# Turning a residual to tokens on partitions: tensor-engine transposes, or VectorE 32x32 transposes with DMAs through DRAM

## The chip, the core and the metric

The kernel runs on one core of a Trainium2 chip. The metric is the device time of one execution in microseconds; the runs shown before the change have a median of 2171.61 us (three runs, 2171.5 to 2172.09).

Engine names are those of the profile: PE is the tensor engine's matmul and PEld its weight load, DVE is VectorE, ACT is ScalarE, POOL is GpSimd, SP is the engine that issues most DMAs. Each engine works through its own instructions in a fixed order. Where an instruction waits, everything behind it on that engine waits too.

## What is computed

A decoder trunk of two residual layers on 256 tokens of width 2048, in float32. The second layer is what matters here:

```python
h = h + odd_mixer(rms_norm(h, mix_norm_w[1]), ...)
f = conv_ffn(rms_norm(h, ffn_norm_w[1]), ...)      # silu(conv(hn @ w_gate)) * (hn @ w_up) @ w_down
h = h + f
return rms_norm(h, final_norm_w)
```

`w_gate` and `w_up` are 2048 x 5632, `w_down` is 5632 x 2048. The output has tokens on the rows.

## The kernel before, in words

**The residual.** `h` stays in SBUF in four tiles `h0` to `h3` (`self.hq`), each of 128 partitions by 4 x 256 floats. Through most of the program a partition is a channel and the 256 columns of a block are tokens. The last down-projection (`finish`) produces tokens on partitions, so before it `h` has to be turned. That is the work of `turn` (L416), a generator that is started with the second layer's FFN (L856) and is not needed until `finish` adds into `h`.

**The products.** Gate and up (`products`, L263) are made of 44 jobs of 256 output channels, each of four weight panels of 512 KB; this text numbers the panels of the second layer from 0. Panels 0 to 7 are the first gate job and the first up job, alternating; from then on a job is four panels in a row: 8 to 11 gate, 12 to 15 up, 16 to 19 gate, 20 to 23 up, 24 to 27 gate, 28 to 31 up, and so on. For a panel, SP loads `raw` (L165, four buffers), ACT rounds it to its high part in `hl` (L167, three buffers), DVE computes the low part as the difference (L168), and PE runs sixteen matmuls (L243): for each of two accumulators and four slices of the panel, one with the high part over 512 columns and one with the low part over 256.

**Behind a job.** Each accumulator is emptied by `total`: ACT copies its upper half (`ev`, L302), DVE adds the lower half (L303). A gate job goes on with a DVE multiplication into a padded tile `pad` (L869), ACT's scaling `cv` (L872), two DVE steps of the convolution (L873, L874), ACT's SiLU (L875) and POOL's multiplication (L876). An up job goes on with DVE's product with that `cv` (L886) and with the split into `act` (ACT L388, DVE L389).

**What sets the order.** `tick` (L292) advances every waiting generator by one step after each panel. The order in which instructions then stand on each engine is not that of the source alone: a scheduler of the framework places them when the program is built, by the order of the source and its own costs. A changed step can so move its neighbours.

**The norm.** `token_scale` runs behind panel 2 (statistics, L335) and panel 4 (broadcast on PE, L343); between them DVE has a chain of ten small steps (L319 to L325).

**The turn before.** From the thirteenth tick on, every fourth tick turns one 128-token half of one tile:

```python
for i in range(4):
    self.nc.tensor.transpose(ps[:, i * P : (i + 1) * P], block[:, i], self.ident)
self.nc.scalar.copy(block, ps.rearrange("p (i c) -> p i c", c=P))
```

That is four 128x128 transposes on PE (L425) into one PSUM bank and one ACT copy back over the block (L426), eight times.

Of the kernel before, what the change touches and what calls it, by code (L numbers as in the profile page):

```python
# [9 lines left out]
F32 = mybir.dt.float32  # L10
# [5 lines left out]
P = 128  # L16
T = 256
NT = T // P
# [54 lines left out]
class Trunk:  # L73
# [341 lines left out]

    def turn(self):  # L416

        for _ in range(12):
            yield
        for g in range(WG):  # L420
            for tt in range(NT):
                ps = self.psum()
                block = self.hq[g][:, :, tt * P : (tt + 1) * P]
                for i in range(4):
                    self.nc.tensor.transpose(ps[:, i * P : (i + 1) * P], block[:, i], self.ident)  # L425
                self.nc.scalar.copy(block, ps.rearrange("p (i c) -> p i c", c=P))  # L426
                yield
                yield
                yield
                yield  # L430

    def pair_sums(self, a0, a1, lent=None, lend=False, homes=None):

# [1067 lines left out]
```

## Time and profile before

| | |
|---|---|
| Median of the runs shown | 2171.61 us |
| Time of the profiled execution | 2171.28 us |
| Its span in the profile | 2169.5 us |
| PE busy, share of the span | 100% |
| DVE, ACT busy, share of the span | 77%, 57% |
| Mean granted TensorE clock | 0.999 |

The span is what the profile records of the program's instructions; the 1.8 us between the profiled execution's span and its time lie before and after. In the profile a busy share says how full an engine is. A group's row has the line, the engine, the operation, what it writes and reads, the count, the busy time, the mean duration in ns, and the idle time ahead of it with what ended it. In a timeline the first two numbers are the start and the length of a piece, and a bracket tells how long the engine had been idle and for whom.

### The profile page before, as it was taken

To read this page: it belongs to the slowest core of one execution; us is meant where nothing else is said; L and a number is where in the kernel's file an instruction comes from. 1 tells how busy PE (TensorE), PEld (TensorE's weight loads), DVE (VectorE), ACT (ScalarE), POOL (GpSimd) and SP (SyncE) were. 2 spreads that over 40 slices of the span, in tenths; PEclk is the share of its full clock that TensorE was granted. 3 is DMA by queue.
4 is the path that set the end of the run, shared out by engine and by line. 5 is a ranking of instruction groups with operands and counts; after the bars stand their busy time and mean duration, and the time that the engine had idled before them with its cause. 6 is when DMAs were issued, how large, how long until landed. Compare 5 with 4: busy or idle time off the path is not lost.

```text
span 2169.5 us, 35606 instructions
## 1 busy us (share of the span) xinstructions
PE 2160.1 (100%) x13723; PEld 1948.6 (90%) x13723; DVE 1679.1 (77%) x2712; ACT 1226.6 (57%) x1855; POOL 96.8 (4%) x107
## 2 busy tenths in 40 slices
PE   9999999999999999999999999999999999999998
PEld 8888888888888888899989999888888888888998
DVE  8788776766676668789889998767666666688997
ACT  7556554655555555555556665546555555555554
POOL 0000000101010100000000000000010101000000
PEclk9999999999999999999999999999999999999999
DMA  7754556556655565566555555555555655666665
GB/s 263 235 175 146 175 183 189 191 194 194 195 194 194 194 194 191 191 200 207 186 193 186 185 174 195 166 194 185 186 193 194 194 194 195 194 203 199 210 200 169
DMA packets 117722, 417.65 MB, mean 193 GB/s; under 512 B 13072, under 2 KB 15408, under 8 KB 117552
## 3 DMA queue, kind: packets, MB, share of 16 engines
q1 hardware_dynamic: 116352, 412.48, 58.3%
q8 instruction: 107, 1.75, 0.3%
q0 software_dynamic: 576, 2.10, 0.3%
q10 hardware_dynamic: 624, 0.81, 0.1%
q14 instruction: 63, 0.52, 0.1%
HBM read 413.22 MB, written 2.11 MB: 191 GB/s over the span
## 4 chain that ended last, share of the span: by engine, by line
PE 99%; DVE 0%; DMA 0%; ACT 0%; SPq 0%; issue 0%; DVEq 0%
PE acc L243 68%; PE acc L578 10%; PE acc L527 6%; PE aux L542 4%; PE acc L542 4%; PE acc L253 1%; PE aux L527 1%; PE acc L260 1%; PE acc L204 0%; PE aux L978 0%; PE aux L1010 0%; PE acc L212 0%; PE aux L212 0%; PE aux L1000 0%; DMA raw<-in_wfirst 0%; PE aux L1311 0%
## 5 line engine op out<-in xcount | busy, mean ns | idle before, releaser
L243 PE MATMUL acc<-x,hl 128*128 128x512 f32 (+1 forms) x7680 | 1325.8, 334 | 0.0
L243 PEld LDWEIGHTS acc<-x,hl 128*128 128x128 f32 x7680 | 1158.5, 188 | 150.2 <-issue 0.9
L168 DVE TENSOR_TENSOR hl<-raw,hl 128x1024 fp32r<-128x1024 f32 x687 | 840.2, 1223 | 410.1 <-ACT hl L167 404.3
L167 ACT CAST hl<-raw 128x1024 fp32r<-128x1024 f32 x687 | 721.3, 1050 | 617.0 <-PE acc L243 364.7
L578 PE MATMUL acc<-hl,act 128*128 128x256 f32 x1872 | 223.7, 277 | 0.0
L578 PEld LDWEIGHTS acc<-hl,act 128*128 128x128 f32 x1872 | 218.5, 188 | 0.6
L243 PE MATMUL acc<-o,hl 128*128 128x512 f32 (+1 forms) x1024 | 176.0, 333 | 0.0
L302 ACT COPY ev<-acc 128x256 f32<-128x256 f32 x242 | 89.9, 372 | 149.3 <-PE acc L243 148.3
L243 PEld LDWEIGHTS acc<-o,hl 128*128 128x128 f32 x1024 | 154.4, 188 | 19.9
L876 POOL TENSOR_TENSOR cv<-cv,rbc 128x256 f32<-128x256 f32 x88 | 93.6, 1083 | 852.7 <-ACT cv L875 852.7
L527 PE MATMUL acc<-hl,act 128*128 128x512 f32 x528 | 120.1, 389 | 0.0
L527 PEld LDWEIGHTS acc<-hl,act 128*128 128x128 f32 x528 | 99.0, 188 | 20.5
L303 DVE TENSOR_TENSOR ev<-acc,ev 128x256 f32<-128x256 f32 x242 | 101.1, 420 | 3.5 <-ACT ev L302 1.9
L506 ACT CAST ts<-tf 128x768 fp32r<-128x768 f32 x77 | 64.3, 836 | 45.0 <-DVE tf L503 44.6
L508 DVE TENSOR_TENSOR ts<-tf,ts 128x768 fp32r<-128x768 f32 x77 | 73.3, 952 | 2.3 <-ACT ts L506 2.2
L496 ACT CAST hl<-raw 128x768 fp32r<-128x768 f32 x53 | 44.3, 836 | 29.2 <-issue 12.2
L500 DVE TENSOR_TENSOR tf<-raw 128x512 f32<-128x512 f32 x77 | 53.1, 690 | 9.7 <-DMA raw<-in_wd 7.9
L542 PE MATMUL aux<-ts,x 128*128 128x256 f32 x405 | 54.6, 276 | 0.0
L542 PE MATMUL acc<-hl,act 128*128 128x256 f32 x318 | 53.4, 276 | 0.0
L505 DVE TENSOR_TENSOR hl<-raw,hl 128x768 fp32r<-128x768 f32 x53 | 50.5, 952 | 3.1 <-ACT hl L496 2.3
L542 PEld LDWEIGHTS aux<-ts,x 128*128 128x128 f32 x405 | 49.9, 188 | 0.0
L886 DVE TENSOR_TENSOR ev<-ev,cv 128x256 f32<-128x256 f32 x88 | 38.3, 437 | 10.3 <-POOL cv L876 1.6
(278 smaller groups left out, 1687.9 us busy)
## 6 DMA issues: line engine op xcount, KB each, us to landing
raw<-in_wg SPq DMA_DIRECT2D x176, 512.0 KB, 3.5
raw<-in_wu SPq DMA_DIRECT2D x176, 512.0 KB, 3.5
raw<-in_wd SPq DMA_DIRECT2D x176, 512.0 KB, 4.1
raw<-in_wev SPq DMA_DIRECT2D x76, 512.0 KB, 4.1
raw<-in_wod SPq DMA_DIRECT2D x64, 512.0 KB, 3.9
raw<-in_wevo SPq DMA_DIRECT2D x32, 512.0 KB, 3.8
raw<-in_wodv SPq DMA_DIRECT2D x32, 512.0 KB, 3.6
raw<-in_wodo SPq DMA_DIRECT2D x32, 512.0 KB, 3.6
```

Of the source, the lines that this page charges most:

```text
L167: nc.scalar.copy(hi, raw)
L168: self.lo = nc.vector.tensor_tensor(lo, raw, hi.bitcast(F32), ALU.subtract)
L243: self.mm = self.nc.tensor.matmul(accs[nt][:, :n], hl[w][:, k, nt * P : (nt + 1) * P], xs[k0 + k][:, :n], start=start and k == w == 0, sto ...
L302: nc.scalar.copy(t, acc[:, T:])
L303: nc.vector.tensor_tensor(t, acc[:, :T], t, ALU.add)
L500: v.tensor_tensor(two(blk(f123, 0, 2)), two(blk(raw, 1, 2)), blk(raw, 3).unsqueeze(1).broadcast_to([P, 2, T]), ALU.subtract)
L506: nc.scalar.copy(t123[0], f123)
L508: v.tensor_tensor(t123[1], f123, t123[0].bitcast(F32), ALU.subtract)
L527: self.nc.tensor.matmul(row.rearrange("p (j c) -> p j c", c=T), self.part(a[k], p, tt), self.both(hl, w, k), start=start and i == k == 0, ...
L542: self.nc.tensor.matmul(to, x[p], w[b][q], start=n == 0 and i in start, stop=n == 2 and i in stop, skip_group_check=alone or i in m,)
L578: mm(row[:, j * T : (j + 1) * T] if own is None else own[:, :T], x, w[:, j], start=first, stop=stop and k == 1 and i == 2 and j == halves[-1],
L876: nc.gpsimd.tensor_tensor(c, c, self.rbc, ALU.mult)
```

## The change

`turn` no longer uses PE, PSUM or ACT's copy. For each of the four tiles:

- one DVE instruction (`nc.vector.transpose`, STREAM_TRANSPOSE in the order below) transposes every 32x32 block of the 128 x 1024 tile into a tile `tr`, of which there is one buffer;
- one DMA, issued by ACT, writes `tr` to a DRAM tile `turn` (512 KB);
- three ticks later four DMAs, issued by ACT, read it back so that each 32x32 block comes to its place; each fills 32 partitions of `h` (128 KB) in 1024 pieces of 128 bytes.

```diff
+        nc = self.nc
         for _ in range(12):
             yield
         for g in range(WG):
-            for tt in range(NT):
-                ps = self.psum()
-                block = self.hq[g][:, :, tt * P : (tt + 1) * P]
-                for i in range(4):
-                    self.nc.tensor.transpose(ps[:, i * P : (i + 1) * P], block[:, i], self.ident)
-                self.nc.scalar.copy(block, ps.rearrange("p (i c) -> p i c", c=P))
+            h = self.hq[g].rearrange("p i t -> p (i t)")
+            t = self.t256("tr", 1, 4 * T)
+            nc.vector.transpose(t, h)
+            back = self.dram.tile([P, 4 * T], F32, name=f"turn{g}")
+            nc.scalar.dma_start(back, t)
+            for _ in range(3):
                 yield
-                yield
-                yield
-                yield
+            src = back.rearrange("(p r) (i b c) -> b r i p c", r=32, b=4, c=32)
+            for b in range(4):
+                dst = h[32 * b : 32 * b + 32].rearrange("r (i p c) -> r i p c", p=4, c=32)
+                nc.scalar.dma_start(dst, src[b])
+            yield
```

The scheduler places the new instructions by its own costs, and with them their neighbours on ACT and DVE up to panel 32; from there on all engines stand as before. In the new kernel the lines of the source behind `turn` are three higher (L872 is L875, L875 is L878). The rows below are ACT's; a name's number tells the tiles of one kernel apart.

**Behind panel 19 (the end of a gate job).** Before, in ACT's order, from the cast of panel 19 (`hl_15415`) over those of panels 20, 21 and 22; the two L302 empty the accumulators of panels 16 to 19:

```order
L167 CAST hl_15415<-raw_15414 128x1024
L426 COPY h_88<-aux_15367 128x4x128
L167 CAST hl_15459<-raw_15458 128x1024
L167 CAST hl_15486<-raw_15485 128x1024
L302 COPY ev_15436<-acc_15344 128x256
L302 COPY ev_15446<-acc_15345 128x256
L167 CAST hl_15507<-raw_15506 128x1024
```

Now, again on ACT from the cast of panel 19 (`hl_15416`); panel 20 is `hl_15463`:

```order
L167 CAST hl_15416<-raw_15415 128x1024
L432 DMA h_89<-turn_15371 32x32x32 x2
L302 COPY ev_15436<-acc_15346 128x256
L302 COPY ev_15446<-acc_15347 128x256
L167 CAST hl_15463<-raw_15462 128x1024
L426 DMA turn_15485<-tr_15483 128x1024
```

The casts of panels 20 and 21 stood ahead of the two copies that empty the accumulators of panels 16 to 19; now they stand behind them.

**Behind panel 23 (the end of an up job).** Before, on ACT, from the cast of panel 24 (`hl_15563`); the L302 empty the accumulators of panels 20 to 23:

```order
L167 CAST hl_15563<-raw_15562 128x1024
L167 CAST hl_15590<-raw_15589 128x1024
L302 COPY ev_15548<-acc_15456 128x256
L302 COPY ev_15554<-acc_15457 128x256
L167 CAST hl_15611<-raw_15610 128x1024
L388 CAST act_14856<-ev_15548 128x256
L388 CAST act_14857<-ev_15554 128x256
```

Now, on ACT from the cast of panel 23 (`hl_15530`) to that of panel 24 (`hl_15569`):

```order
L167 CAST hl_15530<-raw_15529 128x1024
L432 DMA h_90<-turn_15485 32x32x32 x2
L302 COPY ev_15550<-acc_15460 128x256
L432 DMA h_90<-turn_15485 32x32x32
L388 CAST act_14856<-ev_15550 128x256
L302 COPY ev_15556<-acc_15461 128x256
L432 DMA h_90<-turn_15485 32x32x32
L388 CAST act_14857<-ev_15556 128x256
L167 CAST hl_15569<-raw_15568 128x1024
```

Here the cast of panel 24 stands behind both copies, two DMAs and both of the job's `act` casts.

**Behind panel 27 (the end of a gate job).** Before, on ACT, from the cast of panel 28 (`hl_15675`):

```order
L167 CAST hl_15675<-raw_15674 128x1024
L167 CAST hl_15702<-raw_15701 128x1024
L302 COPY ev_15652<-acc_15560 128x256
L302 COPY ev_15662<-acc_15561 128x256
L167 CAST hl_15723<-raw_15722 128x1024
L872 ACTIVATE cv_15656<-pad_14899,params 128x256
L872 ACTIVATE cv_15666<-pad_14900,params 128x256
```

Now, on ACT from the cast of panel 27 (`hl_15636`) to those of panels 28 (`hl_15683`) and 29:

```order
L167 CAST hl_15636<-raw_15635 128x1024
L432 DMA h_91<-turn_15591 32x32x32 x2
L302 COPY ev_15656<-acc_15566 128x256
L302 COPY ev_15666<-acc_15567 128x256
L432 DMA h_91<-turn_15591 32x32x32
L875 ACTIVATE cv_15660<-pad_14899,params 128x256
L875 ACTIVATE cv_15670<-pad_14900,params 128x256
L167 CAST hl_15683<-raw_15682 128x1024
L167 CAST hl_15704<-raw_15703 128x1024
```

The cast of panel 28 now follows both copies and both scalings of the job that panel 27 ends.

Three smaller moves, in words. On ACT the cast of panel 9 stood between the copies of panels 0 to 6 and those of panel 7's job; now it stands behind all four copies, and behind it come the table load, the first SiLU, a scaling and the cast of panel 10. On DVE the transposition of `h2` stands between the low part of panel 14 and that of panel 15, and waits for the write of `turn1`, which ACT issues behind the cast of panel 14. On PE each of panels 10, 20, 24 and 28 now begins with two matmuls over 512 columns, one for each accumulator, before the first that needs the low part; before, each began with one.

## Prediction

> **What bounds the kernel now.** I begin with the page: span, engines, and the chain of waits that ended last.
>
> ```profile
> span 2169.5 us, 35606 instructions
> PE 2160.1 (100%) x13723; PEld 1948.6 (90%) x13723; DVE 1679.1 (77%) x2712; ACT 1226.6 (57%) x1855; POOL 96.8 (4%) x107
> PE 99%; DVE 0%; DMA 0%; ACT 0%; SPq 0%; issue 0%; DVEq 0%
> ```
>
> PE never stops, and the chain is PE's own work. Whatever leaves PE shortens the run; whatever makes PE wait lengthens it. Next the stretch in which the transposes stand, by engine, and the transposes by their line:
>
> ```profile
> 1483.00:1563.00 80.00, 80.00 (x481) 71.08 (x481) 53.82 (x80) 45.62 (x72) 7.15 (x8) 1.00 0.57 187
> L425 PE MATMUL aux<-consts,h x32: 272/272/273, 1483.6 to 1563.3; 128*128 128x128 f32 x32
> L426 ACT COPY h<-aux x8: 577/581/582, 1484.8 to 1564.2; 128x512 f32<-128x512 f32 x8
> ```
>
> In these 80 us PE is busy throughout, at a granted clock of 1.00, while DVE works 53.82 us and ACT 45.62: a third of each is free on average. That average is not yet a reason: ACT and DVE prepare the panels, in order. What counts is how early. ACT's timeline around the first transposes:
>
> ```profile
> 1479.75 0.37 ACT L302 COPY ev<-acc 128x256 f32<-128x256 f32 x1 [0.27 <-PE acc L243]
> 1481.11 0.38 ACT L302 COPY ev<-acc 128x256 f32<-128x256 f32 x1 [0.99 <-PE acc L243]
> 1481.38 1.05 ACT L167 CAST hl<-raw 128x1024 fp32r<-128x1024 f32 x1
> 1482.33 0.91 ACT L872 ACTIVATE cv<-pad,params 128x256 f32<-128x256 f32 x2
> 1483.88 1.05 ACT L167 CAST hl<-raw 128x1024 fp32r<-128x1024 f32 x1 [0.64 <-ACT cv L872]
> ```
>
> and PE's timeline:
>
> ```profile
> 1461.77 22.03 PE L243 MATMUL acc<-x,hl 128*128 128x512 f32 x128
> 1483.63 0.60 PE L425 MATMUL aux<-consts,h 128*128 128x128 f32 x4
> 1483.99 11.15 PE L243 MATMUL acc<-x,hl 128*128 128x512 f32 x64
> 1494.97 0.60 PE L425 MATMUL aux<-consts,h 128*128 128x128 f32 x4
> ```
>
> The first transposes follow panel 12, so panel 13 starts at 1483.99. The cast at 1483.88 is panel 15's, by ACT's order. Panel 15 starts two panels after 1483.99, near 1489.4: the cast runs 5.5 us ahead. With three `hl` buffers it cannot run earlier, since the buffer is freed two panels before; with cast and difference it keeps some 3 us in hand. **That lead, not the idle share, is the cover**, and it exists only while the cast stands ahead of the copies for which ACT must wait until a job's last matmul.
>
> **What the change takes from PE.** The chain in order of time gives the price of a group:
>
> ```profile
> 1483.80 0.44 PE aux L425 x4
> 1484.23 10.90 PE acc L243 x64
> 1495.14 0.44 PE aux L425 x4
> ```
>
> Four panels take 10.90 us, or 2.73 each; four transposes 0.44. Eight groups: 8 x 0.44 = **3.5 us saved**. ACT also loses eight copies of 0.58 us, which nothing waits for on PE.
>
> **What it adds in instructions.** Four DVE transpositions, four writes and sixteen reads issued by ACT. The nearest rows:
>
> ```profile
> 1482.46 1.23 DVE L168 TENSOR_TENSOR hl<-raw,hl 128x1024 fp32r<-128x1024 f32 x1
> 1.19 0.45 ACTq L129 DMA_DIRECT2D h<-in_x  x1
> L1230 ACTq DMA_DIRECT2D rows<-s x1: 335/335/335, 82.9 to 82.9; - x1
> raw<-in_wg SPq DMA_DIRECT2D x176, 512.0 KB, 3.5
> out<-x ACTq DMA_DIRECT2D x2, 256.0 KB, 2.7
> sr<-rows POOLq DMA_DIRECT2D x4, 512.0 KB, 6.3
> ```
>
> - *Transposition, 128x1024:* not in the trace. DVE's pass over this shape takes 1.23 us; I take 1.2, with 0.6 and 2.4 (half and twice that row) as ends.
> - *Write of 512 KB:* between 2.7 us (256 KB out) and 6.3; a load of this size lands in 3.5, and beside the loads I take 4.2.
> - *Issue of a read on ACT:* 0.34 us with 32 rows, 0.45 with 128. From 0.34 as the lower end, eight times 0.45 = 3.6 us if it grows with the 1024 pieces. I take 0.5 to 1.0, by the small step between these two rows; ACT's idle time below hides that.
> - *Landing of the reads:* nobody needs `h` for hundreds of microseconds. SP reuses their semaphores several panels later, so even 10 us (over three panels) costs nothing.
> - *Weights beside them:* DMA is 0.57 busy in the row of the stretch. At four buffers a load is issued four panels (10.9 us) ahead of its buffer's next use, so 4 us more for a load stays covered.
>
> **What the moved rows cost.** Here the order decides. Three casts now stand behind copies that wait for the panel directly ahead, so at these places the lead of 5.5 us is gone, and PE stops. Rows for the pieces:
>
> ```profile
> 1480.66 0.42 DVE L303 TENSOR_TENSOR ev<-acc,ev 128x256 f32<-128x256 f32 x1
> 1481.11 0.42 DVE L869 TENSOR_TENSOR pad<-ev,rbc 128x256 f32<-128x256 f32 x1
> 1483.61 0.87 DVE L873 SCALAR_TENSOR_TENSOR cv<-pad,params,cv 128x256 f32<-128x256 f32 x2
> 1492.52 0.42 DVE L886 TENSOR_TENSOR ev<-ev,cv 128x256 f32<-128x256 f32 x1
> 1475.27 0.74 ACT L388 CAST act<-ev 128x256 fp32r<-128x256 f32 x2 [0.56 <-DVE ev L886]
> 1471.57 1.28 ACT L875 ACT_TABLE_LOAD   x1
> 1485.96 1.73 POOL L876 TENSOR_TENSOR cv<-cv,rbc 128x256 f32<-128x256 f32 x2 [11.01 <-ACT cv L875]
> ```
>
> Panel 12 starts 2.73 us before 1483.63, at 1480.90, and the copy of panel 11's job at 1481.11: **0.21 us from a job's last matmul slot to its copy**. The next ACT instruction follows a copy after 0.27 (1481.11 to 1481.38), a difference follows its cast after 0.03 (1482.43 to 1482.46). A wide matmul takes 0.23 us: two thirds of a pair, 10.90/32.
>
> - *Panel 20.* From PE's last slot: 0.21 + 0.27 (copy) + 1.05 (cast) + 0.03 = 1.56 us without a matmul. Then PE has two wide matmuls, 0.45, while the difference takes 1.23 from the cast's end: 0.8 more. **2.4 us.**
> - *Panel 24.* The first half's chain, 0.37 + 0.42 + 0.42 and hand-offs, holds ACT's first L388 and with it the second copy to 0.41 from the slot. Then copy 0.37, L303 0.42, L886 0.42, L388 0.27, cast 1.05 and five hand-offs of 0.03: 3.1. The low part again 0.8. **3.9 us.** ACT idles 0.9 us between copy and L388, in which the issue of a DMA hides.
> - *Panel 28.* 0.21 + copy 0.37 + L303 and two L869 (three of DVE's steps, 1.1 us) + one scaling 0.41 + cast 1.05 and hand-offs: 3.3. The difference stands behind four convolution steps and starts 0.2 after the cast: 1.0 more. **4.3 us.** About 0.55 us of idle ACT hides the DMA between.
> - *Panel 10.* Behind panel 7: 0.21 + 0.27 + cast 0.95 + table 1.28 + SiLU 0.50 + POOL 0.9 to 1.08 bring DVE's L886 to about 4.3, and with the convolution of the other half the difference of panel 10 ends near 6.8. Panel 10 starts at 5.45 and reaches its low part at 5.9. **1.0 us.**
> - *Panel 15.* The transposition of `h2` waits for the write of `turn1`. The write is issued near 6.2 us before panel 15; 4.2 and hand-offs, then 1.2 and 1.23, end about when PE asks. **0.2 us**, up to 2.3 with a landing of 6.3.
>
> After each place ACT gets its lead back within two panels, since it needs 1.56 us of every 2.73 (45.62 of 80). Sum: 2.4 + 3.9 + 4.3 + 1.0 + 0.2 = 11.8 us lost, 3.5 saved: **+8.3 us**. The profiled execution took 2171.28 us, 0.3 under the median of 2171.61; on the median this gives **2179.9 us**.
>
> **Rivals.**
>
> - *Hidden: not slower.* The copies stand early but PE has other matmuls in between, as in panels 0 to 7 where two jobs alternate. Then only the 3.5 us remain: 2168.1. It decides once the five gaps come to less than 3.5 us, under 0.7 each. For it speaks the free third of ACT and DVE; against it, that panel 20 directly follows 19 on PE in both orders, 24 follows 23, 28 follows 27, and ACT cannot pass a waiting copy. Chance 4%.
> - *Dear issue.* If a read holds ACT for 2.5 us, two of them behind panel 23 exceed their idle time of 0.9 by 1.6 each and the one behind 27 its 0.55 by 2.0: some 5 us more, 2185. Rows of 32 and 128 speak against it; 1024 pieces were never seen. Chance 15%. At 3.6 us every group would stall and the time pass 2190.
> - *Late write.* A landing of 6.3 us adds 2 at panel 15 and, by DVE's wait inside the chain of the norm, about 1.5 at panel 5: 2183.5. Chance 8%.
> - *Slow clock after a gap.* The two longest gaps are 3.1 and 3.3 us. The start of the run shows what an idle PE gives:
>
> ```profile
> L177 PE MATMUL aux<-z 128*128 128x128 f32 x16 | 3.8, 431 | 1.1 <-DVE z L174 1.1
> ```
>
> There 16 matmuls of 128 columns take 3.8 us, while the transposes need 0.11 each, so 1.7: 2.0 us are lost. Twice that makes 2184. Against it: the granted clock of the stretch says nothing of gaps, and both gaps are short. Chance 10%. The Trainium skill, "TensorE: Matmul & The Clock Gate", Part 1, has such a rule: an idle window of about 3.4 us halves the clock, and as much busy time restores it. The slow start agrees (431 ns against 272); no run here shows a gap in mid-stream.
>
> - *Fewer places.* One of the three long gaps does not open: 2175.5 to 2177.5. Chance 5%.
>
> **How the numbers follow.** The forecast of order stalls at cheap issues has 58%, its own range 2176 to 2183. The low end takes the waits for the high parts alone (1.56 + 3.1 + 3.3 - 3.5 = +4.5). The high end takes dear issue, or late write and slow clock together, and reaches 2190. Below 2176 and above 2190 I leave about 1 in 10 together with the hidden case. A difference under 0.2% (4.3 us) can hardly be told from no change here; hidden at -3.5 us falls within it. Slower 92%, same 7%, faster 1%.
>
> **What will show it.** PE idle ahead of panels 20, 24 and 28, released by ACT's cast and then DVE's difference, near 2.4, 3.9 and 4.3 us; about 1 us at panel 10; no PE gap from panel 32 on. Reads issued in 0.5 to 1.0 us. The forecast is wrong if PE stays busy there, if the reads hold ACT longer, or if matmuls behind a gap lengthen.

## The result and the profile after

| | before | changed kernel |
|---|---|---|
| Median of six runs each | 2171.56 us (2171.25 to 2172.09) | 2185.06 us (2184.57 to 2186.38) |
| Ratio, 95% interval | | 1.0062 [1.0052, 1.0072] |
| Span of the profiled execution | 2169.5 us | 2182.9 us |
| Mean granted clock | 0.999 | 0.996 |

The change costs 13.5 us; 8.3 were forecast. The page of the changed kernel, first lines and chain:

```profile
span 2182.9 us, 35563 instructions
PE 2163.8 (99%) x13691; PEld 1948.4 (89%) x13691; DVE 1684.6 (77%) x2716; ACT 1223.7 (56%) x1847; POOL 101.4 (5%) x107
PE 98%; DVE 1%; ACT 0%; DMA 0%; issue 0%; SPq 0%; POOL 0%; DVEq 0%; ACTq 0%; POOLq 0%
```

PE now runs 32 matmuls fewer and is busy 3.7 us longer, and the span grew by 13.4: there are waits, and the matmuls themselves also take longer. PE's timeline has every wait of the stage in its brackets:

```profile
1461.91 14.35 PE L243 MATMUL acc<-x,hl 128*128 128x512 f32 x82
1476.97 27.07 PE L243 MATMUL acc<-x,hl 128*128 128x256 f32 x158 [0.71 <-DVE hl L168]
1505.51 0.73 PE L243 MATMUL acc<-x,hl 128*128 128x512 f32 x2 [1.46 <-ACT hl L167]
1506.83 10.77 PE L243 MATMUL acc<-x,hl 128*128 128x256 f32 x62 [0.59 <-DVE hl L168]
1520.83 14.12 PE L243 MATMUL acc<-x,hl 128*128 128x512 f32 x64 [3.23 <-ACT hl L167]
1538.13 1.22 PE L243 MATMUL acc<-x,hl 128*128 128x512 f32 x2 [3.19 <-ACT hl L167]
1539.65 80.53 PE L243 MATMUL acc<-x,hl 128*128 128x256 f32 x461 [0.29 <-DVE hl L168]
```

The gaps stand at panels 10, 20, 24 and 28: at panel 10 for the difference (DVE) alone, at 20 and 28 for the cast (ACT) and two matmuls later for the difference, at 24 for the cast. The piece of 64 matmuls behind panel 24's gap shows the second loss: four panels take 14.12 us in this view, and the four before it (2 + 62) needed 0.73 + 10.77. Why is in the windows of the same kernel; columns are the stretch, its length, PE's busy time and matmuls, the granted clock, the DMA share and GB/s:

```profile
1515.00:1520.00 5.00, 2.60 (x16) 0.99 0.80 197
1520.00:1521.00 1.00, 0.17 (x1) 0.50 0.70 283
1521.00:1524.00 3.00, 2.96 (x8) 0.50 0.52 164
1524.00:1526.00 2.00, 2.00 (x8) 0.50 1.14 244
1526.00:1527.00 1.00, 1.00 (x6) 0.64 0.87 307
1527.00:1532.00 5.00, 5.00 (x32) 1.00 1.05 278
...
1540.00:1543.00 3.00, 3.00 (x11) 0.50 0.76 239
1543.00:1544.00 1.00, 1.00 (x6) 0.61 0.80 291
1544.00:1549.00 5.00, 5.00 (x31) 1.00 0.60 203
```

By the 0.99 of the first row the clock falls to half near 1519.9, still inside the gap; 0.64 in the microsecond from 1526 puts its return near 1526.7. PE worked from 1520.83 to 1526.7, 5.9 us, at half speed: 2.9 us lost. The gap at panel 28 does the same, with full speed back near 1543.8: 5.6 us, another 2.8, part of which falls on the wait for the difference. Both spells of half clock last 6.8 us (1519.9 to 1526.7, and 1537.0 to 1543.8 by the trace's record of the clock).

Counted by slots (start to start, less the 0.23 or 0.11 us that a matmul takes in a row), the waits are 0.9, 2.5, 3.4 and 4.4 us at panels 10, 20, 24 and 28, in sum 11.2. (What PE lost behind the first two matmuls, 1.1 us at panel 28, is counted there; at panel 24 it is 0.8 and is left to the slow clock.) With some 5 us of slow clock and the 3.5 saved that is +12.7 of the 13.4 us; 0.7 are left.

The new instructions in the changed kernel's trace, by their lines (the transposition and the issue of the reads, ns min/median/max):

```profile
L424 DVE STREAM_TRANSPOSE tr<-h x4: 1236/1238/1243, 1452.9 to 1510.5; 128x1024 f32<-128x1024 f32 x4
L432 ACTq DMA_DIRECT2D h<-turn x16: 564/565/707, 1458.3 to 1535.0; - x16
```

and its DMAs, with KB each and median us from issue to landing:

```profile
turn<-tr ACTq DMA_DIRECT2D x4, 512.0 KB, 3.5
h<-turn ACTq DMA_DIRECT2D x16, 128.0 KB, 4.9
```

None of them is dear. What costs is where their presence put ACT's casts; ACT's timeline behind panel 23, before:

```profile
1512.45 1.05 ACT L167 CAST hl<-raw 128x1024 fp32r<-128x1024 f32 x1 [1.67 <-PE acc L243]
1513.77 0.37 ACT L302 COPY ev<-acc 128x256 f32<-128x256 f32 x1 [0.27 <-PE acc L243]
1515.13 0.37 ACT L302 COPY ev<-acc 128x256 f32<-128x256 f32 x1 [0.99 <-PE acc L243]
1515.40 1.05 ACT L167 CAST hl<-raw 128x1024 fp32r<-128x1024 f32 x1
```

and at the same place in the changed kernel:

```profile
1516.27 0.37 ACT L302 COPY ev<-acc 128x256 f32<-128x256 f32 x1 [5.75 <-PE acc L243]
1517.67 0.40 ACT L388 CAST act<-ev 128x256 fp32r<-128x256 f32 x1 [1.02 <-DVE ev L889]
...
1519.73 2.93 ACT L167 CAST hl<-raw 128x1024 fp32r<-128x1024 f32 x3
```

ACT stands 5.75 us at the first copy with a cast ready behind it, and then makes up three casts in a row.

### The profile page after: what moved, and what is told of

Read it like the earlier page. It is cut to its first block, busy times and chain, and to the rows that moved or that the text cites. A ratio compares the mean times of both kernels' runs of the same rounds, so it can differ in the third digit from the quotient of the medians.

```text
span 2182.9 us, 35563 instructions
## 1 busy us (share of the span) xinstructions
PE 2163.8 (99%) x13691; PEld 1948.4 (89%) x13691; DVE 1684.6 (77%) x2716; ACT 1223.7 (56%) x1847; POOL 101.4 (5%) x107
## 4 chain that ended last, share of the span: by engine, by line
PE 98%; DVE 1%; ACT 0%; DMA 0%; issue 0%; SPq 0%; POOL 0%; DVEq 0%; ACTq 0%; POOLq 0%
PE acc L243 68%; PE acc L581 10%; PE acc L530 5%; PE aux L545 4%; PE acc L545 4%; PE acc L253 1%; PE aux L530 1%; PE acc L260 1%; PE acc L204 0%; PE aux L981 0%; PE aux L1013 0%; PE acc L212 0%; PE aux L212 0%; PE aux L1003 0%; DMA raw<-in_wfirst 0%; PE aux L1314 0%
## 5 line engine op out<-in xcount | busy, mean ns | idle before, releaser
L302 ACT COPY ev<-acc 128x256 f32<-128x256 f32 x242 | 90.1, 373 | 165.0 <-PE acc L243 159.0
L879 POOL TENSOR_TENSOR cv<-cv,rbc 128x256 f32<-128x256 f32 x88 | 98.2, 1134 | 861.2 <-ACT cv L878 861.2
```

Of the source, the lines that this page charges most:

```text
L302: nc.scalar.copy(t, acc[:, T:])
L879: nc.gpsimd.tensor_tensor(c, c, self.rbc, ALU.mult)
```

## The experiments

"Before" was run on the same chip beside each: medians of 2171.3 to 2171.9 us, and none of its 76 executions over 2174.6.

**Is it the reads, and does it matter who issues them?** Four kernels, each the changed one with one edit. In e1 the reads are left out; in e2 GpSimd issues them; in e3 one more step lies between two reads; in e4 SP issues them.

```diff
             for b in range(4):
                 dst = h[32 * b : 32 * b + 32].rearrange("r (i p c) -> r i p c", p=4, c=32)
-                nc.scalar.dma_start(dst, src[b])
+                pass                                  # e1
+                nc.gpsimd.dma_start(dst, src[b])      # e2
+                nc.sync.dma_start(dst, src[b])        # e4
```

> Leaves out: the sixteen reads from DRAM, so the residual enters the last sum unturned. The transpositions and writes stay. ACT's order is then that of before: every cast stands two panels ahead of its use. Theory A (the moved casts make PE wait, and the long waits slow its clock): no PE gap in panels 9 to 31, granted clock 1.00 throughout, 3.5 us saved, some 2168 us. Theory B (VectorE's transpositions and ACT's writes cost the time): stays near 2185. Theory C (the reads cost it by themselves, as traffic or as ACT's time): also about 2168, so this run tells B apart, not A from C.

> The whole change, but the sixteen reads are issued by POOL in place of ACT. ACT's casts then stand as before the change, while the same 16384 pieces of 128 bytes cross the same DMA engines. Theory A: no PE gap behind panels 19, 23 and 27, clock 1.00, 3 to 3.5 us under the kernel before: about 2168.3 us. Theory C as traffic: weights late, PE gaps of some us, 2175 or more. Theory C as ACT's time: also about 2168.

> Reads stay on ACT, one more tick between each two of them. In the order built so the cast of panel 36 alone stands behind copies that wait for the panel before, beside the smaller move at panel 10. Theory A: a gap of about 1.6 and 0.9 us at panel 36 and 1.0 at panel 10, no gap long enough to slow the clock: 3.5 saved against 3.6 lost, 2171 to 2173 us. Theory C (ACT held by sixteen issues of 0.56 us, or traffic): the same number of issues and bytes as in the change, so near 2185.

> The sixteen reads are issued by SP, ACT issues the four writes only. In the order built so the casts of panels 20, 24 and 28 stand behind the copies as in the change, although no read stands on ACT. Theory A: gaps of about 2.0, 3.4 and 3.4 to 5.6 us in front of the three panels, granted clock 0.5 behind the last two for 5 to 6 us each; about 2186 us (2183 to 2189). Theory C as ACT's time: back to about 2168, since ACT issues none of them.

e1: 2169.15 us, ratio 1.0002 [0.9986, 1.0018]; eight of ten executions lie between 2168.4 and 2170.6, two at 2182.4 and 2184.2. The gaps at the panels are gone (PE waits 0.64 us once, ahead of L343), and what is left is nearly the saving of the eight transposes. e4: 2189.71 (one execution; 2183 to 2189 was expected). ACT issues no read there, and yet the gaps are there, PE's timeline of e4:

```profile
1505.95 0.74 PE L243 MATMUL acc<-x,hl 128*128 128x512 f32 x2 [1.82 <-ACT hl L167]
1523.21 0.73 PE L243 MATMUL acc<-x,hl 128*128 128x512 f32 x2 [3.19 <-ACT hl L167]
1542.46 7.82 PE L243 MATMUL acc<-x,hl 128*128 128x512 f32 x25 [5.45 <-ACT hl L167]
```

So the time ACT spends on issuing the reads is not the cause; the casts stand behind the copies in e4 too. (The clock fell behind all three of e4's gaps, for 3.4, 3.4 and 6.8 us.) e3: 2180.69 us, ratio 1.0041 [1.0020, 1.0062], three executions from 2171.8 to 2175.3 and three from 2186.1 to 2189.1, where 2171 to 2173 was expected. Its gaps moved to other panels (0.63, 1.99 and 1.41 + 0.58 us); its profiled execution, the slowest, has half clock for 3.4 us behind the last of them and then the slow pace that e2 shows next. In e2 the casts stand ahead of the copies again and PE waits at none of these panels, but the median is 2183.54 us, ratio 1.0046 [1.0030, 1.0063], with five of six executions from 2182.2 to 2185.7 and one at 2171.45. This no theory had expected. e2's profile has the clock at 1.00 throughout the stage, and in the stretch from 1600 to 1900 us, matmuls by their shape:

```profile
L243 PE MATMUL acc<-x,hl 128*128 128x512 f32 x858 | 300.3, 395 | 0.0
L243 PE MATMUL acc<-x,hl 128*128 128x256 f32 x858 | 240.7, 281 | 0.0
```

Before has there:

```profile
L243 PE MATMUL acc<-x,hl 128*128 128x512 f32 x883 | 300.3, 389 | 0.0
L243 PE MATMUL acc<-x,hl 128*128 128x256 f32 x884 | 244.2, 276 | 0.0
```

The same pair of matmuls takes 350 ns in place of 340, without a wait and at full clock. From 1465 to 1944 us that is some 1,370 pairs by 10.5 ns, 14 us. In e2 it begins at a wait:

```profile
1457.92 5.71 PE L243 MATMUL acc<-x,hl 128*128 128x512 f32 x32
1464.62 0.71 PE L343 MATMUL aux<-consts,rcol 128*128 128x128 f32 x4 [0.99 <-DVE rcol L325]
```

The slow pace is no product of the change. Before has it in the first layer: its wide matmuls are at the fast pace from 42 to 80 us (first row) and at the slow one from 83 to 118 us (second row), behind a few other matmuls and without a wait:

```profile
L243 PE MATMUL acc<-x,hl 128*128 128x512 f32 x113 | 38.5, 389 | 0.0
...
L243 PE MATMUL acc<-x,hl 128*128 128x512 f32 x100 | 35.2, 396 | 0.0
```

Hence Theory P: behind an interruption the pairs may go on at the other pace and keep it.

**Is the order on ACT enough by itself?** e6 is before, the residual turned by PE, with only three casts held back; e7 and e9 do that at eight places each, so that the gaps differ in length.

```diff
+        kind = None
+        if self.panel is not None:
+            kind = (lambda n: {20: "ev", 24: "act", 28: "cv"}.get(n))(self.panel)
+            self.panel += 1
+        with ExitStack() as held:
+            if kind is not None:
+                held.enter_context(self.tc.issue_after(self.held[kind].ins))
+            nc.scalar.copy(hi, raw)
...
+            kind = (lambda n: "act" if n in range(24, 88, 8) else None)(self.panel)   # e7
+            kind = (lambda n: "ev" if n in range(20, 84, 8) else None)(self.panel)    # e9
```

> Before, with the residual still turned by PE, and only the casts of panels 20, 24 and 28 forced behind the accumulator copy, the activation's cast and the convolution's scaling of the panel ahead of them, as they stand in the changed kernel. Theory A (the order on ScalarE is what costs, and the slow clock after the two longer gaps): PE waits about 1.0, 3.8 and 4.8 us, in sum 9.5, the granted clock falls to 0.50 after the second and third and costs some 5 us more: 2186, and 573 matmuls in 100 us nowhere after it, or 14 us more where they are. Theory B (the transfers of the residual cost the time): 2171.6, no gap.

e6: 2185.55 us, ratio 1.0073 [1.0051, 1.0095]; three executions from 2184.1 to 2186.1, one at 2193.9. With no transposition by VectorE and no transfer of the residual, the time is that of the changed kernel. Its parts are others: e6 keeps the 3.5 us of PE's transposes, its waits come to 8.0 us in the profile (the gap at panel 20 is short here), and one spell of half clock follows. So it is luck that the two times agree so closely; what e6 shows is that the order alone makes the gaps. PE's timeline of e6 (its lines are nine higher here):

```profile
1506.79 0.74 PE L252 MATMUL acc<-x,hl 128*128 128x512 f32 x2 [0.18 <-ACT hl L176]
1522.29 0.74 PE L252 MATMUL acc<-x,hl 128*128 128x512 f32 x2 [2.79 <-ACT hl L176]
1523.55 10.76 PE L252 MATMUL acc<-x,hl 128*128 128x256 f32 x62 [0.52 <-DVE hl L177]
1538.06 0.89 PE L252 MATMUL acc<-x,hl 128*128 128x512 f32 x2 [3.74 <-ACT hl L176]
```

Behind the gap of 2.79 + 0.52 us the 62 matmuls run at full speed; only behind that of 3.74 does the clock fall. It was expected behind both.

> Before, with the cast of panel 24 and of every eighth panel after it (to 80) forced behind the cast of the activation; eight gaps of some 3.4 + 0.8 us. Theory A (waits, and a clock that falls some 2.2 us into a gap): waits of 31.7 us in sum, the granted clock at 0.50 after seven or eight of the gaps at 2.5 to 3 us each, 20 us more: 2221 to 2226. Theory W (only the waits count, the slow clock was an accident of two gaps): 2203.

e7: 2216.03 us (2213.2 to 2224.8), ratio 1.0209 [1.0185, 1.0232]; 2221 to 2226 was expected. Seven of its gaps are 3.2 + 0.5 us and the first, with twenty of PE's transposes ahead of it, 1.32 + 0.53. The waits come to 28.1 us in the profile, and the clock falls at every one of the eight gaps. Around the second of them:

```profile
1542.00:1546.00 4.00, 0.77 (x4) 1.00 0.00 0
1546.00:1547.00 1.00, 0.48 (x3) 0.95 0.00 0
1547.00:1550.00 3.00, 3.00 (x11) 0.50 0.79 209
1550.00:1551.00 1.00, 1.00 (x6) 0.84 0.70 274
1551.00:1555.00 4.00, 4.00 (x25) 1.00 0.55 193
```

The slow spell lasts from 1546.9 to 1550.3, 3.4 us, half of that in the changed kernel. Theory W (waits alone, 2203) is out: the profiled execution, the slowest, is 53 us over before, and of these 28 are waits, some 15 the slow clock (eight spells at half speed, together nine times 3.4 us) and some 7 the slow pace, which it took behind its last gap (574 matmuls in 100 us at a clock of 1.00, for 246 us); some 3 are left. The fastest execution is still 41 us over before. There is no transfer of the residual and no transposition by VectorE in this kernel, so Theory Q, that the pace needs one of them, is out as well.

> Before, with the cast of panel 20 and of every eighth panel after it (to 76) forced behind the accumulator copy of the panel ahead; eight gaps of some 1.8 us and 0.5 to 1 us more two matmuls later, against 3.2 and 0.5 in e7. Theory A (the clock falls only in a gap of over some 2.2 us): 18 to 22 us of waits, no stretch at a granted clock of 0.50: 2190 to 2194, or up to 12 us more in executions that take the slow pace of 350 ns a pair. Theory T (every gap of about 2 us costs the slow clock too): 20 us more, 2210 to 2216.

e9: 2201.37 us (2200.5 to 2202.2), ratio 1.0134 [1.0117, 1.0151], between the two theories: 18.2 us of waits, and the clock falls behind four of the eight gaps (the first of which is short, 0.18 + 0.23 us). The third gap of e9 and then the fourth, each 1.82 + 0.78 us on the page:

```profile
1558.28 0.74 PE L252 MATMUL acc<-x,hl 128*128 128x512 f32 x2 [1.82 <-ACT hl L176]
1559.79 21.63 PE L252 MATMUL acc<-x,hl 128*128 128x256 f32 x126 [0.78 <-DVE hl L177]
1583.24 0.74 PE L252 MATMUL acc<-x,hl 128*128 128x512 f32 x2 [1.82 <-ACT hl L176]
1584.76 23.76 PE L252 MATMUL acc<-x,hl 128*128 128x256 f32 x126 [0.78 <-DVE hl L177]
```

The same gap costs nothing more the first time and 2.1 us the second (a spell at half clock, and some 100 matmuls at the slow pace). Length alone does not decide. The trace's record of the clock shows what differs: in it all changes of the clock lie whole multiples of 3.413 us apart, and on this grid the fourth gap fills most of one step (1581.8 to 1585.2, PE busy for 0.35 of it), while the third is spread over two (PE busy for 0.58 and 0.66).

**What starts the slow pace?** e5 and e10 are before with one wait at the norm's matmuls; in e5 they come one step earlier, in e10 the norm iterates eight times.

```diff
-        self.bg.append(self.token_scale(sums, 2, 2))
+        self.bg.append(self.token_scale(sums, 2, 1))                                # e5
+        self.bg.append(self.token_scale(sums, 2, 2, 3 if out is None else 8))       # e10
...
-        for _ in range(3):
+        for _ in range(self.newton):                                                # e10
```

> Before, with one number changed: the four matmuls of the norm (L343) come one step (16 matmuls, 2.7 us) earlier, so that PE waits for rcol; no transposition by VectorE, no DMA of the residual, no moved cast. Theory P (after an interruption of PE's chain of paired matmuls the pairs settle at one of two paces, 339.5 or 350 ns, and keep it to the end of the stage at about 1945 us): the wait itself gives 0.8 to 1.5 us, and the time is either near 2172.5 or, where the slow pace is taken, some 1400 pairs by 10.5 ns = 14.7 us more, near 2187; in the profile the stretches of 100 us from 1600 on hold 590 or 573 matmuls. Theory Q (the slow pace came from the residual's DMAs or VectorE's transpositions): 590 in all stretches, every execution near 2172.5.

> Before, with eight steps of Newton's iteration in place of three for the norm ahead of the second layer's gate and up products (the value stays the same), so that L343's matmuls come when rcol isn't ready: one gap of about 1 us on PE, where e5's came out too short to count (some 0.2 us); nothing else is changed, no transposition or transfer is added, no cast moved. Theory P (a gap by itself lets the pairs go on at 339.5 or at 350 ns): about 2172.8 in some executions and 14 to 15 us more, near 2187, in others, the granted clock 1.00 in both. Theory Q (the slow pace needs the residual's transfers, VectorE's transpositions or a fall of the clock): every execution near 2172.8.

e5: 2171.93 us, ratio 1.0002 [0.9993, 1.0012]; its gap was too small to show. e10: 2172.36, ratio 1.0004 [0.9994, 1.0013], a gap of 0.58 us; all ten executions lie between 2172.0 and 2173.6. So not every wait changes the pace, and Theory P in its plain form missed.

**A version without the waits.** e8 and e12 are one kernel, run on two chips: the changed one with the reads on GpSimd and the norm's matmuls one step later (in both layers). e11 is e2 again, on the chip of e12.

```diff
-                nc.scalar.dma_start(dst, src[b])
+                nc.gpsimd.dma_start(dst, src[b])
...
-        self.bg.append(self.token_scale(sums, 2, 2))
+        self.bg.append(self.token_scale(sums, 2, 3))
```

> The changed kernel with the reads issued by GpSimd, as in e2, and L343's matmuls one step later, so that PE waits nowhere in the stage. Theory P (the slow pace of e2 began at its gap of 0.99 us ahead of L343): no gap, 590 matmuls in each 100 us, and the 3.5 us of PE transpositions saved: 2168, faster than both kernels. Theory Q (the slow pace comes from transfers or transpositions): near 2183 as e2.

> The kernel of e2 once more, now beside that of e8 on one chip, since e2 and e8 ran on different chips. Theory P (the gap ahead of L343 lets the pairs take the slow pace): a gap of about 1 us there, most executions near 2183, the profile at 573 matmuls in 100 us where its time is near 2183 and at 590 where it is near 2170. Theory C (the slow executions of e2 were the chip's): all near 2169 to 2170.

> The kernel of e8 once more, on the chip of e11. Theory P: no gap in the stage, every execution 2168 to 2170, also where e11 shows executions near 2183. Theory C: as e11, within 1 us of it.

e8: 2168.64 us, ratio 0.9985 [0.9976, 0.9995], all ten executions between 2167.4 and 2170.2. e12: 2168.34, ratio 1.0003 [0.9982, 1.0024]: seven executions between 2167.4 and 2169.0, and three from 2181.3 to 2183.0. e11: 2182.15, ratio 1.0024 [1.0002, 1.0046]: six from 2181.8 to 2183.7, four from 2168.2 to 2169.8. So Theory P, which expected none at the slow pace in e12, missed there too. (Where executions fall into two groups, the median says which is the larger, and the ratio lies between.) The profiled execution of e12 took the slow pace, so PE's timeline shows the start:

```profile
1469.71 46.54 PE L243 MATMUL acc<-x,hl 128*128 128x512 f32 x267
1516.66 83.58 PE L243 MATMUL acc<-x,hl 128*128 128x256 f32 x476 [0.41 <-DVE hl L168]
```

and windows of e12 from both sides of it and later:

```profile
1492.00:1515.00 23.00, 23.00 (x137) 1.00 0.97 221
1518.00:1541.00 23.00, 23.00 (x133) 1.00 0.70 220
1600.00:1700.00 100.00, 100.00 (x573) 1.00 0.59 187
```

Again the lasting change of pace stands at a wait, now of 0.41 us ahead of a panel: 137 matmuls in 23 us ahead of it, 133 behind it, and 573 in 100 us later. (Around 1485 the pace had been slow for 10 us already, without a wait that the profile shows.) e8's profile has no wait in the stage and 590 there. In all, judged by their times, e2 and e11 took the slow pace in 11 of 16 executions, e8 and e12 in 3 of 20. The version is faster than both kernels in 17 of its 20 executions, by about 3 us against before and 16 against the changed one; over both chips it is not shown to be faster than before.

## Why the prediction was right, and where it was short

**The saving.** 3.5 us of PE's transposes: e1 stands 2.6 us under before and e8 3.1, in the medians. Nearly all of it arrives once nothing waits.

**The moved casts.** The heart of the forecast. By panels, forecast and measured: 10, 1.0 (0.9 by its own terms, 6.8 less 5.9) and 0.9; 20, 2.4 and 2.5; 24, 3.9 and 3.4; 28, 4.3 and 4.4; 15, 0.2 and nothing (panel 24's low part did cost its 0.8, but under the slow clock, and is counted there). The sum was 11.8 and is 11.2, the places are the forecast ones, and no gap follows panel 28. That order alone does this is shown by e6, from the other side: gaps at panels 24 and 28 without any part of the residual's new way.

**The new operations.** Transposition 1.24 us for 1.2; write landing 3.5 for 4.2; issue of a read 0.565 for 0.5 to 1.0; landing 4.9, for which PE did not wait. (The profile puts one wait of ACT, for the copy at 1502.72, down to a landing; the accumulator that it copies was finished at 1502.69.) "Dear issue" and "late write" fell with these numbers, and e4 shows besides that the issue of the reads on ACT is not what makes the gaps. The "hidden" rival would have been about right for e1 and e8, where the casts keep their place.

**The step that failed** is "Slow clock after a gap", kept out of the sum with "both gaps are short" and given 10%. It is a term of the sum: both long gaps brought a spell of half clock of 6.8 us each, some 5 us together, and that is nearly all of the difference between 8.3 and 13.5. The prediction's own last sign of being wrong, that matmuls behind a gap lengthen, came true. The rival had the mechanism, at 4.1 us, and its 2184 comes within 1.1 us of the result. The result lies above the forecast's own range of 2176 to 2183; the whole range reached it because its upper end, 2190, was made for dear issue, or for a late write together with the slow clock. That it held is partly luck. The rule of the Trainium skill ("TensorE: Matmul & The Clock Gate", Part 1) that stood beside it counts the activity in windows of about 3.4 us, and the traces agree with this: the slow spells last 3.4 us (e7, e9) or 6.8 (the changed kernel, and one of e7's). They do not agree that the window must be idle as a whole: in e9 gaps of 1.82 and 0.78 us with two matmuls between them were enough, in three of six cases.

**What stays open.** What makes the pace of 350 ns a pair begin at one wait and not at another; whether VectorE's transpositions or the transfers make it likelier (before, e5 and e10 have no execution at such a time; e1, with the transpositions and the writes alone, has two of ten); and why the framework's scheduler puts the casts behind the copies with the reads on ACT or SP and not with them on GpSimd.

## What to carry to other kernels

Look at what a change does to the order on the engines that feed the bound one, before the price of its instructions: three casts behind copies cost three times what the change could save, and in e8's profile the sixteen DMAs make PE wait nowhere. A gap on PE of 2 to 3 us may cost half of 3.4 or 6.8 us on top, for the clock: of the gaps of about 1.8 + 0.8 us in e9 three of six did, of those of about 3.2 us all. And when a kernel comes in two times some 14 us apart at a full clock, count matmuls in equal stretches and look at the place where the count drops: in e2, e11 and e12 the lasting drop stands at a wait.

## What was not expected of the hardware

- A pair of matmuls (512 and 256 columns) has two paces, 340 and 350 ns (590 and 573 matmuls in 100 us), at a granted clock of 1.00. In the traces of e2, e11 and e12 a pace, once taken behind a wait of 0.3 to 1.0 us, lasted more than 400 us, and cost 12 to 14 us; e10's wait of 0.58 us left it alone in ten executions.
- The slow clock comes in spells of 3.4 or 6.8 us. A gap of 2.79 + 0.52 us brought none in e6, one of 1.82 + 0.78 brought one in some of e9's cases. In each of the fourteen traces every change of the clock, from the first rise to the fall at the end of the work, lies a whole number of steps of 3.413 us from the others. Every step at full clock in which PE was busy for less than 0.44 of the time ended in a fall, none with over 0.51 did, and of the four between two did (PE's busy time is partly modelled). By this e6's gap lies over two steps, of 0.44 and 0.59.
- The issue of a read of 1024 pieces took ACT 0.565 us; on GpSimd it took 0.97 (e2).
